# An f32 encoder layer on one core: rows for the MLP turned in 32x32 blocks by VectorE instead of by TensorE transposes

## The chip, the core and the metric

The kernel runs on one core of one Trainium2 chip. Its time is the device time of one execution in microseconds (us); the median of several runs is given, with the lowest and highest. A core has five engines that matter here, each with a queue of its own that it runs in order: TensorE (PE in the profile; its weight loads are PEld), VectorE (DVE), ScalarE (ACT), GpSimd (POOL) and SyncE (SP, which only issues transfers). ScalarE and GpSimd issue transfers too.

## The reference

One layer over two sequences, a prompt of 1024 rows and a sample of 512 rows, 1024 wide, all in f32:

```
xn = RMSNorm(x);  z = xn @ W_in -> q_A,k_A,v_A,q_B,k_B,v_B,gate_A,gate_B
A  = grouped-query attention (8 heads of 64, 2 key heads), 2-D rotary
B  = 2-D neighbourhood attention, learned position bias
x  = x + (sigmoid(gate_A) * (o_A @ W_pA) + sigmoid(gate_B) * (o_B @ W_pB)) @ W_out
x  = x + relu(RMSNorm(x) @ W_up)^2 @ W_down          (1024 -> 4096 -> 1024)
out = RMSNorm(x)
```

The change touches the RMSNorm ahead of the MLP and the way its result gets from rows to columns: `RMSNorm(x) @ W_up` needs the normalised rows with the 1024 features on the partitions, while the norm itself has rows on the partitions.

## The kernel before

Every f32 product is made of three products of a reduced form (`mm3`): each operand is cut in a high part (a copy by ScalarE) and a low part (x minus the copy, by VectorE), and hi·hi, hi·lo and lo·hi are added up in PSUM. So each operand tile costs one ScalarE pass and one VectorE pass.

The two sequences go one after the other through the same phases (`run`, one `Trunk` each: s0 is the sample, s1 the prompt): projections and attention A, attention B, and a last phase with the merge and the product with W_out. Then `mlp` runs over all 1536 rows, in two blocks of 768 rows. Its up projection uses a Strassen-Winograd scheme: the activation block is cut in 2x2 parts, of which seven combinations `B[0]` to `B[6]` are made once per block, and seven combinations of the weights (`A`, from sums called `S`) for each of the blocks of the 4096 features. The seven products go to the PSUM banks `ua`, `ub`, `uc`, `ud`.

The last phase of a trunk works on tiles of 128 rows, in two column halves. In half 1 each tile ends like this: TensorE finishes `ops` (the product with W_out), VectorE adds the residual (`hs`, L1389), and `norm_tile` makes the normalised tile: ScalarE squares and sums, VectorE scales the mean (`ms_hs`, L176), GpSimd takes the power (`rs_hs`, L180), and VectorE multiplies row by its factor and by the gain (`xnhs`, one SCALAR_TENSOR_TENSOR over 128x1024, L291). GpSimd stores the tile to a DRAM buffer `hnd`.

- In s0 the phase has four tiles, and each round also normalises one tile of the next trunk: `xnns`, the same steps, which TensorE then turns with eight transposes into `ptxs` (`p0_t`, L315); ScalarE and VectorE cut that into `xs_0h` and `xs_0l` (L331). The next trunk's projections (`zs`, weights `wghs` and `wgls`) begin right behind.
- In s1 there are eight tiles; the first four are normalised in the phase, the other four later, one at a time, inside the up loop of block 0 (`late_norm`).

`hnd` is read back on SP's queue, two tiles of 128 rows at a time (rows j and j+3 of a block of six), and `pair_t` makes one column strip of all seven `B[i]` from such a pair: 16 TensorE transposes (L355) turn the two tiles into four PSUM banks (`pt`), ScalarE copies one of them aside (`y`, L372), VectorE makes the four temporaries `ta` (L377 to L383), and ScalarE and VectorE (two of the low parts GpSimd) write the high and low parts (L364, L367). Block 0's three pairs are made in rounds 3 to 5 of s1's last phase, between the products with W_out; block 1's three pairs between block 0's and block 1's up loops, beside the first down products (`dnf`).

A scheduler (the Tile framework) turns the program into one order per engine, with semaphores where a value or a buffer is waited for, from its own estimates; the order in the code is a starting point for it. Names in the profile leave out the buffer numbers.

Of the kernel before, what the change touches and what calls it, by code (L numbers as in the profile page):

```python
# [11 lines left out]
F32 = mybir.dt.float32  # L12
# [49 lines left out]
def encoder(ctx: ExitStack, tc: tile.TileContext, xs, outs, w):  # L62
# [217 lines left out]

    def norm_tile(src, gb, pool, nm, tag="xn", bufs=2, pin=False, between=None):

        xn = pool.tile([P, D], F32, tag=tag, name=f"xn{nm}", bufs=bufs)
        ss = sml.tile([P, 8], F32, tag="ss", name=f"ss{nm}")
        op = nc.scalar.activation(xn, src, AF.Square, accum_out=ss[:, 0:1])
        if pin:
            tc.keep_in_program_order(op)
        r = rstd(ss[:, 0:1], 1, D, nm, pin)
        if between is not None:
            between()  # L290
        op = nc.vector.scalar_tensor_tensor(xn, src, r[:, 0:1], gb, op0=ALU.mult, op1=ALU.mult)  # L291
        if pin:
            tc.keep_in_program_order(op)
        return xn

    def norm_to(xn, src, gb, nm, pin=False):
# [4 lines left out]
        r = rstd(ss[:, 0:1], 1, D, nm, pin)  # L301
        op = nc.vector.scalar_tensor_tensor(xn, src, r[:, 0:1], gb, op0=ALU.mult, op1=ALU.mult)
        if pin:
            tc.keep_in_program_order(op)
        return xn
# [43 lines left out]

    def pair_t(nm, j, tiles, B, banks, tmp):  # L350

        b11, b21, b12, b22 = banks
        for halves, t in (((b11, b21), tiles[0]), ((b12, b22), tiles[1])):
            for c in range(NC8):
                nc.tensor.transpose(  # L355
                    halves[c // 4][:, (c % 4) * P : (c % 4 + 1) * P], t[:, c * P : (c + 1) * P], ident
                )
        cols = slice(j * P, (j + 1) * P)

        def v(t):  # L360
            return t.rearrange("p (k c) -> p k c", c=P)

        def hi(i, src):
            nc.scalar.activation(B[i][:, 0, :, cols], v(src), AF.Copy)  # L364

        def lo(i, src, eng=nc.vector):
            eng.tensor_tensor(B[i][:, 1, :, cols], v(src), B[i][:, 0, :, cols].bitcast(F32), op=ALU.subtract)  # L367

        y1 = tmp(f"y1{nm}")
        a2, a1, a3, a4 = (tmp(f"ta{i}{nm}") for i in (2, 1, 3, 4))  # L370
# [9 lines left out]
        nc.vector.tensor_tensor(a3, b22, y1, op=ALU.subtract)  # L380
# [40 lines left out]
    def run(tr, nxt, first):  # L421
# [854 lines left out]
        with phase(f"phG{N}") as ph:  # L1276
# [5 lines left out]
            def tmp_zs(name):  # L1282
                return ph.tile([P, 512], F32, tag="zs", name=name, bufs=6 if nxt is not None else 8)

            def hn_raw(j):
                res = []
                for t in (j, j + 3):
                    r = rawp.tile([P, 1024], F32, tag="raw", name=f"hn0_{t}")
                    nc.sync.dma_start(r, hnd[t * P : (t + 1) * P, :])
                    res.append(r)  # L1290
                return res

            def pool_wp(shape, dt, name):
                return ph.tile(shape, dt, tag="k4", name=name, bufs=4)

# [46 lines left out]
            for half in range(2):  # L1342
                wo = wos[half]
                hc = slice(half * 512, half * 512 + 512)
                for tt in range(NT):
# [6 lines left out]
                    if later:  # L1352
                        xr = ph.tile([P, D], F32, tag="k4", name=f"xr{nm}", bufs=4)[:, 0:512]
                    else:
                        xr = tmp_zs(f"xr{nm}")
                    nc.sync.dma_start(xr, x[tt * P : (tt + 1) * P, hc])
                    ht = hs_[tt // 2][:, tt % 2, :] if tb == 0 else None
                    if ht is None and half == 1 and not later:
                        ht = ph.tile([P, D], F32, tag="k4", name=f"ht{nm}", bufs=4)
                        nc.sync.dma_start(ht[:, 0:512], hd[rows_, 0:512])  # L1360
                    if half == 1 and nxt is not None:
                        xt = ph.tile([P, D], F32, tag="k4", name=f"xa{nm}", bufs=4)
                        nc.sync.dma_start(xt, nxt.x[tt * P : (tt + 1) * P, :])
# [36 lines left out]
                    if half == 1:  # L1400
                        if later:
                            late_norms.append(r0)
                        else:
                            hn = norm_tile(ht, gb, ph, f"h{nm}", "k4", 4)
                            nc.gpsimd.dma_start(hnd[rows_, :], hn)
                        if nxt is not None:

                            if tt < NT - 1:
                                ahead.append((tt, norm_tile(xt, gn, ph, f"n{nm}", "k4", 4)))
                            else:  # L1410
                                xn = slot_left([P, D], F32, f"xnn{nm}")
                                nxt.carry.append((tt, norm_to(xn, xt, gn, f"n{nm}")))
                        else:
                            if tt == 2:
                                hn_t = hn_raw(0)
                            if tt == 3:

                                right.close()
# [5 lines left out]
                            if 3 <= tt <= 5:  # L1424
                                j = tt - 3
                                if j == 2:
# [3 lines left out]
                                    first_a0.append(a0)  # L1430
                                both = [big(f"pt0_{j}_{i}") for i in range(2)]
                                banks = [b_[:, q * 512 : q * 512 + 512] for b_ in both for q in range(2)]
                                pair_t(f"0_{j}", j, hn_t, B0, banks, tmp_zs)
                                if j < 2:
                                    hn_t = hn_raw(j + 1)
            if nxt is not None:
                nxt.ready = NT

    def mlp():
# [27 lines left out]
        def hn_load(b, j):  # L1467
            res = []
            for t in (j, j + 3):
                r0 = b * BT + t * P  # L1470
                r = raw4(f"hn{b}_{t}")
                nc.sync.dma_start(r, hnd[r0 : r0 + P, :])
                res.append(r)
            return res
# [300 lines left out]
        for q in range(3):  # L1775
            if q < 2:
                for g in range(2):
                    a_dma(5, g, q + 1)
            pair_t(f"1_{q}", q, hn.pop(q), B, [bank(f"pt1_{q}_{i}") for i in range(4)], t2)
            if q < 2:  # L1780
# [208 lines left out]
```

## Time and profile before

| | |
|---|---|
| median of 3 runs | 2117.03 us (2116.83 to 2118.7) |
| the profiled execution | 2116.56 us, of which its span is 2114.6 us |
| granted TensorE clock | 0.999 of full speed |
| `pair_t`: TensorE transposes | 96, in six groups of 16 |
| tiles normalised for the MLP | 12: four in s0's last phase (from 357 us), four in s1's (from 1132 us), four in block 0's up loop |

In the tables that follow, a group row gives line, engine, operation, output <- inputs, shapes and count, then busy time and mean ns of one, then the idle time of the engine just before these instructions and what ended most of it. A timeline row gives start, duration (both us), engine, line, operation; a bracket at its end is the idle time before it and its releaser. Matmuls overlap in the pipeline, so TensorE's work is read from start to start. A row of a stretch gives its window, its length, and then the busy time and count of TensorE, its weight loads, VectorE, ScalarE and GpSimd, and the granted clock, the share of the transfer engines and GB/s. A row for L1094 by length gives the count, then shortest, median and longest in ns.

### The profile page before, as it was taken

Reading aid. Unit: us, or ns where it says so; the run is one execution under the profiler, and the core shown is the slowest. Engines: PE = TensorE matmul, PEld = TensorE weight load, DVE = VectorE, ACT = ScalarE, POOL = GpSimd, SP = SyncE. Lnnn points to the kernel's source line nnn. Section 1 sums busy time; section 2 is a strip of 40 time slices with the busy share of each in tenths; the row PEclk is TensorE's granted clock in tenths of the full one; section 3 lists DMA queues with packets and bytes.
Section 4 is the critical chain, followed back from the end, with each engine's and each line's share of the span. In section 5 each row is a group of like instructions: output and inputs, shape, how many; then the busy total and the mean of one; then the engine's idle time right before and its main releaser. Section 6 shows DMA issues by size and latency. Waiting matters only on the chain.

```text
span 2114.6 us, 31728 instructions
## 1 busy us (share of the span) xinstructions
PE 2092.2 (99%) x10871; PEld 1838.6 (87%) x10871; DVE 1478.7 (70%) x2793; ACT 1146.4 (54%) x2487; POOL 361.8 (17%) x446
## 2 busy tenths in 40 slices
PE   9999999999999999999999999999999999999998
PEld 8888788988898888888888999999999988888887
DVE  6665786777647756778863877777777777669563
ACT  6664653667566645556522566566555633334442
POOL 2232310333233314543101100012000000000000
PEclk9999999999999999999999999999999999999999
DMA  6437557530132136776563565478444899688561
GB/s 192 135 104 213 147 168 253 177 85 26 55 83 69 43 99 196 234 238 200 166 218 133 184 200 197 156 234 221 154 160 146 281 354 338 214 280 279 156 208 61
DMA packets 336104, 372.92 MB, mean 176 GB/s; under 512 B 31039, under 2 KB 267207, under 8 KB 335943
## 3 DMA queue, kind: packets, MB, share of 16 engines
q1 hardware_dynamic: 297463, 305.60, 45.9%
q10 hardware_dynamic: 31328, 45.11, 6.4%
q0 software_dynamic: 7152, 20.19, 3.5%
q8 instruction: 86, 1.41, 0.3%
q14 instruction: 75, 0.61, 0.1%
HBM read 274.29 MB, written 97.32 MB: 176 GB/s over the span
## 4 chain that ended last, share of the span: by engine, by line
PE 78%; DVE 1%; issue 1%; ACT 0%; POOL 0%; DMA 0%; POOLq 0%; DVEq 0%; ACTq 0%
PE dn L214 20%; PE gpss L214 8%; PE ud L214 6%; PE ua L214 6%; PE uc L214 6%; PE ops L214 3%; PE ub L214 3%; PE pTs L835 3%; PE zs L214 2%; PE ppbs L214 2%; PE pqbs L214 2%; PE pkbs L214 2%; PE ppas L214 2%; PE zvs L214 2%; PE dnf L214 2%; PE os L811 1%
## 5 line engine op out<-in xcount | busy, mean ns | idle before, releaser
L214 PE MATMUL dn<-wd,ah 128*128 128x512 f32 x1248 | 384.1, 389 | 0.0
L214 PEld LDWEIGHTS dn<-wd,ah 128*128 128x128 f32 x1248 | 234.3, 188 | 48.3
L214 PE MATMUL dn<-wd,al 128*128 128x512 f32 x624 | 242.8, 389 | 0.0
L1463 ACT ACTIVATE ah<-ar 128x512 fp32r<-128x512 f32 x168 | 104.5, 628 | 208.4 <-PE dn L214 193.2
L214 PE MATMUL gpss<-xs_0h,w_gs 128*128 128x512 f32 x512 | 189.6, 402 | 0.7 <-DVE ot_Bs L477 0.4
L1464 DVE TENSOR_TENSOR al<-ar,ah 128x512 fp32r<-128x512 f32 x168 | 114.2, 686 | 78.6 <-ACT ah L1463 71.3
L214 PE MATMUL ud<-B,A 128*128 128x384 f32 x768 | 143.6, 334 | 0.7 <-DVE c L1581 0.7
L214 PE MATMUL uc<-B,A 128*128 128x384 f32 x768 | 143.7, 334 | 0.0
L214 PE MATMUL ua<-B,A 128*128 128x384 f32 x768 | 138.8, 334 | 0.0
L214 PEld LDWEIGHTS dn<-wd,al 128*128 128x128 f32 x624 | 117.2, 188 | 24.5
L799 POOL TENSOR_SCALAR ps<-ps,rls 128x1024 f32<-128x1024 f32 (+1 forms) x96 | 97.4, 1016 | 227.6 <-DVE rls L798 209.6
L214 PEld LDWEIGHTS ud<-B,A 128*128 128x128 f32 x768 | 133.9, 188 | 1.0 <-DVE c L1581 1.0
L214 PEld LDWEIGHTS uc<-B,A 128*128 128x128 f32 x768 | 134.0, 188 | 0.2 <-ACT A L1463 0.2
L214 PEld LDWEIGHTS ua<-B,A 128*128 128x128 f32 x768 | 133.7, 188 | 0.2
L841 DVE TENSOR_TENSOR ptls<-pTs,pths 128x512 fp32r<-128x512 f32 x160 | 107.8, 686 | 36.5 <-ACT pths L840 35.5
L840 ACT ACTIVATE pths<-pTs 128x512 fp32r<-128x512 f32 x160 | 94.3, 598 | 69.1 <-PE pTs L835 66.6
L214 PE MATMUL ops<-wh_os,mgs 128*128 128x512 f32 x384 | 119.5, 391 | 0.0
L793 DVE TENSOR_REDUCE nms<-ss 128x1 f32<-128x1024 f32 (+1 forms) x96 | 99.4, 1039 | 20.1 <-PE ss L791 19.0
L214 PEld LDWEIGHTS gpss<-xs_0h,w_gs 128*128 128x128 f32 x512 | 96.1, 188 | 18.9 <-DVE w_gs L208 0.7
L796 ACT ACTIVATE ps<-ss,nms 128x1024 f32<-128x1024 f32 (+1 forms) x96 | 93.3, 972 | 31.5 <-DVE nms L793 29.0
L180 POOL TENSOR_TENSOR rs_f<-ms_f,mhalf 128x1 f32<-128x1 f32 x6 | 4.0, 666 | 590.7 <-DVE ms_f L176 590.7
L835 PEld LDWEIGHTS pTs<-ident,ps 128*128 128x128 f32 x640 | 78.3, 140 | 27.6 <-POOL ps L799 4.0
(287 smaller groups left out, 5137.9 us busy)
## 6 DMA issues: line engine op xcount, KB each, us to landing
ar<-ud SPq DMA_DIRECT2D x120, 512.0 KB, 5.1
br<-in_w_mlp_down_dram SPq DMA_DIRECT2D x72, 512.0 KB, 5.4
rawu<-in_w_mlp_up_dram SPq DMA_DIRECT2D x64, 512.0 KB, 4.1
ud<-c ACTq DMA_DIRECT2D x128, 192.0 KB, 2.9
raw_gs<-in_w_in_dram SPq DMA_DIRECT2D x32, 512.0 KB, 3.9
ud<-cs SPq DMA_DIRECT2D x64, 192.0 KB
tbs<-pbs SPq DMA_DIRECT2D x24, 384.0 KB, 4.6
bhs<-tbs SPq DMA_DIRECT2D x24, 384.0 KB, 3.8
```

The source lines that it names most:

```text
L180: op = nc.gpsimd.tensor_tensor(r[:, :n], m[:, :n], mhalf[:, :n], op=ALU.pow)
L214: op = nc.tensor.matmul(out, a, b, **kw)
L793: nc.vector.tensor_reduce(nm_, s, axis=AX.X, op=ALU.max, negate=True)
L796: op = nc.scalar.activation(p, s, AF.Exp, bias=nm_, accum_out=l)
L799: nc.gpsimd.tensor_scalar(p, p, rl, 1.0, op0=ALU.mult, op1=ALU.mult)
L811: nc.tensor.matmul(o, vhl[:, kc, :], lo, start=False, stop=(kc == NT - 1))
L835: nc.tensor.transpose(pt[:, j * P : (j + 1) * P], PP[u, j][:, kc * P : (kc + 1) * P], ident)
L840: nc.scalar.activation(hi, pt, AF.Copy)
L841: nc.vector.tensor_tensor(lo, pt, hi.bitcast(F32), op=ALU.subtract)
L1463: nc.scalar.activation(hi, src, AF.Copy)
L1464: nc.vector.tensor_tensor(lo, src, hi.bitcast(F32), op=ALU.subtract)
```

## The change

The 96 transposes go. A tile is turned in two steps. VectorE turns each 32x32 block in place with a STREAM_TRANSPOSE (`turned`), and the load that reads the tile back from `hnd` puts the blocks in their places (`turned_rows`): it takes pieces of 256 f32 (1 KB), 512 of them, where it took 128 whole rows of 4 KB. So that each piece holds what one partition needs, the scaling pass of the norm now reads its row and the gain with a stride of four f32 (`blocked`) and writes contiguously. `pair_t` reads the loaded tiles directly, in runs of 32 elements; its banks and the copy `y` are gone. All twelve tiles are turned so. Around it, the loads for block 0 are issued in rounds 1 to 3, into two kinds of buffers; the last phase of s1 has five buffers of the kind `k4` (four before), and six of the kind `zs` (eight before).

```
-    def norm_tile(src, gb, pool, nm, tag="xn", bufs=2, pin=False, between=None):
+    def blocked(t, natural):
+        return t.rearrange("p (c i b) -> p b c i" if natural else "p (b c i) -> p b c i", b=4, i=32)
+
+    def norm_tile(src, gb, pool, nm, tag="xn", bufs=2, pin=False, between=None, turn=False):
...
+        if turn:
+            nc.vector.scalar_tensor_tensor(
+                blocked(xn, False), blocked(src, True), r[:, 0:1], blocked(gb, True), op0=ALU.mult, op1=ALU.mult
+            )
+            turned(xn)
+            return xn
...                                                    (the same in norm_to)
-    def pair_t(nm, j, tiles, B, banks, tmp):
-
-        b11, b21, b12, b22 = banks
-        for halves, t in (((b11, b21), tiles[0]), ((b12, b22), tiles[1])):
-            for c in range(NC8):
-                nc.tensor.transpose(
-                    halves[c // 4][:, (c % 4) * P : (c % 4 + 1) * P], t[:, c * P : (c + 1) * P], ident
-                )
+    def turned(xn):
+
+        blocks = xn.rearrange("p (n i) -> p n i", i=32)
+        nc.vector.transpose(blocks, blocks)
+
+    def turned_rows(r0):
+        return hnd[r0 : r0 + P, :].rearrange("(a i) (b w) -> (i b) a w", i=32, b=4)
+
+    def pair_t(nm, j, tiles, B, tmp):
+
+        (b11, b21), (b12, b22) = (
+            [t.rearrange("p (a c t) -> p c a t", a=4, c=8)[:, 4 * h : 4 * h + 4] for h in range(2)] for t in tiles
+        )
...
-        nc.scalar.activation(y1, b12, AF.Copy)
...
-        nc.vector.tensor_tensor(a1, y1, b11, op=ALU.subtract)
+        nc.vector.tensor_tensor(a1, b12, b11, op=ALU.subtract)
...
-            def hn_raw(j):
-                res = []
-                for t in (j, j + 3):
-                    r = rawp.tile([P, 1024], F32, tag="raw", name=f"hn0_{t}")
-                    nc.sync.dma_start(r, hnd[t * P : (t + 1) * P, :])
...
+            def hn_raw(j, e):
+                if j and e:
+                    r = ph.tile([P, D], F32, tag="k4", name=f"hn0_{j}_{e}", bufs=nk4)
+                else:
+                    r = rawp.tile([P, 1024], F32, tag="raw", name=f"hn0_{j}_{e}")
+                nc.sync.dma_start(r.rearrange("p (a w) -> p a w", a=4), turned_rows((j + 3 * e) * P))
...
-                            hn = norm_tile(ht, gb, ph, f"h{nm}", "k4", 4)
+                            hn = norm_tile(ht, gb, ph, f"h{nm}", "k4", nk4, turn=True)
...
-                            if tt == 2:
-                                hn_t = hn_raw(0)
+                            if tt == 1:
+                                hn_raw(0, 0)
+                                hn_raw(0, 1)
+                                hn_raw(1, 0)
+                            if tt == 2:
+                                hn_raw(1, 1)
+                            if tt == 3:
+                                hn_raw(2, 1)
...                                                    (rounds 3 to 5; mlp)
-            norm_to(xn, hl.pop(r0), gl[0][:, 0, :], f"l{r0}")
+            norm_to(xn, hl.pop(r0), gl[0][:, 0, :], f"l{r0}", turn=True)
```

The engines' orders move with it at three places that matter. A name ends in half, tile and buffer number; `xnhs_1_0` is the normalised tile 0 of half 1.

VectorE's order in s0's last phase, before:

```order
L291 SCALAR_TENSOR_TENSOR xnhs_1_0_4455<-hs_0_4284,rs_hs_1_0_4460,gbms_4286 128x1024
L176 TENSOR_SCALAR ms_ns_1_0_4467<-ssns_1_0_4465 128x1
L1389 TENSOR_TENSOR hs_0_4284<-ops_1_1_4476,xrs_1_1_4472 128x512
L291 SCALAR_TENSOR_TENSOR xnns_1_0_4464<-xas_1_0_4426,rs_ns_1_0_4469,gns_4288 128x1024
L176 TENSOR_SCALAR ms_hs_1_1_4523<-sshs_1_1_4521 128x1
L291 SCALAR_TENSOR_TENSOR xnhs_1_1_4520<-hs_0_4284,rs_hs_1_1_4525,gbms_4286 128x1024
L176 TENSOR_SCALAR ms_ns_1_1_4532<-ssns_1_1_4530 128x1
L331 TENSOR_TENSOR xs_0l_4503<-ptxs_0_4505,xs_0h_4501 128x4x128
L331 TENSOR_TENSOR xs_0l_4504<-ptxs_0_4505,xs_0h_4502 128x4x128
L291 SCALAR_TENSOR_TENSOR xnns_1_1_4529<-xas_1_1_4474,rs_ns_1_1_4534,gns_4288 128x1024
```

and after:

```order
L295 SCALAR_TENSOR_TENSOR xnhs_1_0_4455<-hs_0_4284,rs_hs_1_0_4460,gbms_4286 128x1024
L176 TENSOR_SCALAR ms_ns_1_0_4468<-ssns_1_0_4466 128x1
L368 STREAM_TRANSPOSE xnhs_1_0_4455<-xnhs_1_0_4455 128x1024
L300 SCALAR_TENSOR_TENSOR xnns_1_0_4465<-xas_1_0_4426,rs_ns_1_0_4470,gns_4288 128x1024
L1411 TENSOR_TENSOR hs_0_4284<-ops_1_1_4477,xrs_1_1_4473 128x512
L176 TENSOR_SCALAR ms_hs_1_1_4524<-sshs_1_1_4522 128x1
L295 SCALAR_TENSOR_TENSOR xnhs_1_1_4521<-hs_0_4284,rs_hs_1_1_4526,gbms_4286 128x1024
L346 TENSOR_TENSOR xs_0l_4504<-ptxs_0_4506,xs_0h_4502 128x4x128
L346 TENSOR_TENSOR xs_0l_4505<-ptxs_0_4506,xs_0h_4503 128x4x128
L368 STREAM_TRANSPOSE xnhs_1_1_4521<-xnhs_1_1_4521 128x1024
L176 TENSOR_SCALAR ms_ns_1_1_4534<-ssns_1_1_4532 128x1
L1411 TENSOR_TENSOR hs_1_4285<-ops_1_2_4543,xrs_1_2_4539 128x512
```

The turn stands ahead of `xnns`, the residual add of the next tile has moved behind `xnns`, and an add and two rows of the next projection's weights (`wgls`) now come ahead of the second `xnns`. On TensorE, the first group of `ptxs` transposes now stands behind five instead of ten matmuls of the third tile's `ops`, and the second behind nineteen instead of eight of the fourth's.

VectorE's order from the fourth tile of s1 to the first pair, before:

```order
L1389 TENSOR_TENSOR hs_1_12581<-ops_1_3_12960,xrs_1_3_12958 128x512
L176 TENSOR_SCALAR ms_hs_1_3_12990<-sshs_1_3_12988 128x1
L291 SCALAR_TENSOR_TENSOR xnhs_1_3_12987<-hs_1_12581,rs_hs_1_3_12992,gbms_12582 128x1024
L367 TENSOR_TENSOR B_0_13000<-pt_0_0_13012,B_0_13000 128x4x128
L377 TENSOR_TENSOR ta_0_13032<-y_0_13030,pt_0_0_13012 128x512
```

and after:

```order
L368 STREAM_TRANSPOSE xnhs_1_2_12957<-xnhs_1_2_12957 128x1024
L396 TENSOR_TENSOR ta_1_13080<-hn_1_1_12967,hn_1_0_12926 128x512
L1411 TENSOR_TENSOR hs_1_12585<-ops_1_3_12971,xrs_1_3_12969 128x512
L398 TENSOR_TENSOR ta_1_13079<-hn_1_1_12967,ta_1_13080 128x512
L176 TENSOR_SCALAR ms_hs_1_3_13001<-sshs_1_3_12999 128x1
L295 SCALAR_TENSOR_TENSOR xnhs_1_3_12998<-hs_1_12585,rs_hs_1_3_13003,gbms_12586 128x1024
L368 STREAM_TRANSPOSE xnhs_1_3_12998<-xnhs_1_3_12998 128x1024
L387 TENSOR_TENSOR B_0_13014<-hn_0_0_12922,B_0_13014 128x4x128
L387 TENSOR_TENSOR B_4_13018<-hn_0_1_12924,B_4_13018 128x4x128
```

One temporary of the second pair (`ta_1`) has come ahead of the add, a second one behind it; the first pair's rows follow the last turn.

TensorE's order at the end of that tile, before:

```order
L214 MATMUL ops_1_3_12960<-wh_os_1_4_12627,mgs_0_4_1_12395 128x512
L355 MATMUL pt_0_0_13012<-ident,hn_0_12954 128x128 x8
L355 MATMUL pt_0_1_13013<-ident,hn_3_12956 128x128 x8
L214 MATMUL ops_1_4_13060<-wh_os_1_0_12615,mgs_1_0_0_12235 128x512
L214 MATMUL ops_1_4_13060<-wl_os_1_0_12616,mgs_1_0_0_12235 128x512
```

and after:

```order
L214 MATMUL ops_1_3_12971<-wl_os_1_4_12632,mgs_0_4_0_12398 128x512
L214 MATMUL ops_1_3_12971<-wh_os_1_4_12631,mgs_0_4_1_12399 128x512
L214 MATMUL ops_1_4_13052<-wh_os_1_0_12619,mgs_1_0_0_12239 128x512
L214 MATMUL ops_1_4_13052<-wl_os_1_0_12620,mgs_1_0_0_12239 128x512
```

The two groups of eight transposes are gone from between the products of two tiles; nothing takes their place.

More of the change, by code (lines that the diff above doesn't have):

```diff
@@ L294, in norm_tile, with norm_to @@
         return xn
-    def norm_to(xn, src, gb, nm, pin=False):
+    def norm_to(xn, src, gb, nm, pin=False, turn=False):
         ss = sml.tile([P, 8], F32, tag="ss", name=f"ss{nm}")
@@ L301, in norm_to @@
         r = rstd(ss[:, 0:1], 1, D, nm, pin)
+        if turn:
+            nc.vector.scalar_tensor_tensor(
+                blocked(xn, False), blocked(src, True), r[:, 0:1], blocked(gb, True), op0=ALU.mult, op1=ALU.mult
+            )
+            turned(xn)
+            return xn
         op = nc.vector.scalar_tensor_tensor(xn, src, r[:, 0:1], gb, op0=ALU.mult, op1=ALU.mult)
@@ L376, in pair_t @@
         lo(0, b11)
[L377 removed]
+        nc.vector.tensor_tensor(a1, b12, b11, op=ALU.subtract)
         hi(2, a1)
         nc.vector.tensor_tensor(a2, b22, a1, op=ALU.subtract)
[L380 removed]
+        nc.vector.tensor_tensor(a3, b22, b12, op=ALU.subtract)
         hi(3, a3)
@@ L1352, in run @@
                     if later:
-                        xr = ph.tile([P, D], F32, tag="k4", name=f"xr{nm}", bufs=4)[:, 0:512]
+                        xr = ph.tile([P, D], F32, tag="k4", name=f"xr{nm}", bufs=nk4)[:, 0:512]
                     else:
@@ L1408, in run @@
                             if tt < NT - 1:
-                                ahead.append((tt, norm_tile(xt, gn, ph, f"n{nm}", "k4", 4)))
+                                ahead.append((tt, norm_tile(xt, gn, ph, f"n{nm}", "k4", nk4)))
                             else:
@@ L1430, in run @@
                                     first_a0.append(a0)
[L1431 to L1435, printed above, removed]
+                                pair_t(f"0_{j}", j, [hn_t[j][e] for e in range(2)], B0, tmp_zs)
+                                if j == 0:
+                                    hn_raw(2, 0)
             if nxt is not None:
@@ L1471, in hn_load @@
                 r = raw4(f"hn{b}_{t}")
-                nc.sync.dma_start(r, hnd[r0 : r0 + P, :])
+                nc.sync.dma_start(r.rearrange("p (a w) -> p a w", a=4), turned_rows(r0))
                 res.append(r)
@@ L1778, in mlp @@
                     a_dma(5, g, q + 1)
-            pair_t(f"1_{q}", q, hn.pop(q), B, [bank(f"pt1_{q}_{i}") for i in range(4)], t2)
+            pair_t(f"1_{q}", q, hn.pop(q), B, t2)
             if q < 2:
```

27 lines of the change are left out of this document (15 added, 12 removed).

## The prediction

> **What bounds the kernel now.** I read the busy shares first, then the chain that ended last.
>
> ```profile
> PE 2092.2 (99%) x10871; PEld 1838.6 (87%) x10871; DVE 1478.7 (70%) x2793; ACT 1146.4 (54%) x2487; POOL 361.8 (17%) x446
> PE 78%; DVE 1%; issue 1%; ACT 0%; POOL 0%; DMA 0%; POOLq 0%; DVEq 0%; ACTq 0%
> ```
>
> TensorE is busy 99% of the span of 2114.6 us, and of the chain's attributed time nearly all is its own. So TensorE work taken out counts in full, as long as nobody is late to TensorE at that place; VectorE work put in counts only where TensorE waits for VectorE. The case is therefore decided at the places where the new VectorE work lies.
>
> **What is removed.** The 96 transposes of `pair_t`, in six groups of 16. Their price is read from the starts of the matmuls around them, since a busy time of pipelined work overlaps its neighbours.
>
> ```profile
> L355 PE MATMUL pt<-ident,hn 128*128 128x128 f32 x96 | 11.6, 273 | 0.0
> 1148.29 0.40 PE L214 MATMUL ops<-wh_os,mgs 128*128 128x512 f32 x1
> 1148.52 1.91 PE L355 MATMUL pt<-ident,hn 128*128 128x128 f32 x16
> 1150.19 0.47 PE L214 MATMUL ops<-wh_os,mgs 128*128 128x512 f32 x1
> 1150.50 0.39 PE L214 MATMUL ops<-wl_os,mgs 128*128 128x512 f32 x1
> 1158.02 0.39 PE L214 MATMUL ops<-wl_os,mgs 128*128 128x512 f32 x1
> 1158.40 1.94 PE L355 MATMUL pt<-ident,hn 128*128 128x128 f32 x16
> 1424.07 1.91 PE L355 MATMUL pt<-ident,hn 128*128 128x128 f32 x16
> 1425.74 0.70 PE L214 MATMUL dnf<-wd,ah 128*128 128x512 f32 x2
> ```
>
> A matmul starts every 0.23 (1148.29 to 1148.52). From 1148.52 to 1150.50 stand 16 transposes and one matmul: 1.98 − 0.23 = 1.75. The second group starts 0.38 after the last matmul, 0.15 more than the pitch. Six groups: 6 x 1.75 + 0.15 = **10.6 us off TensorE**. From below 6 x 1.67 = 10.0 (1424.07 to 1425.74), from above the busy time of the group, 11.6. The 1.67 is 0.104 for one transpose.
>
> [...]
>
> `pair_t` also drops its ScalarE copy (y1) and waits for nothing from TensorE now; both lie beside TensorE work and are costed at nothing, for ScalarE is 54% busy.
>
> **What is added, per turned tile.** (a) The scaling pass (SCALAR_TENSOR_TENSOR, below STT) reads both sources at a stride of four f32, 16 bytes; (b) a new 32x32 STREAM_TRANSPOSE of 128x1024 on VectorE. Twelve tiles, four each in three places.
>
> ```profile
> L291 DVE SCALAR_TENSOR_TENSOR xnhs<-hs,rs_hs,gbms 128x1024 f32<-128x1024 f32 x8 | 10.3, 1285 | 5.3 <-POOL rs_hs L180 5.3
> L1106 DVE STREAM_TRANSPOSE pbs<-pbs 128x768 f32<-128x768 f32 x24 | 23.2, 966 | 0.0
> L1389 DVE TENSOR_TENSOR hs<-ops,xrs 128x512 f32<-128x512 f32 x16 | 10.8, 687 | 23.5 <-PE ops L214 23.5
> L1094 ACT ACTIVATE pbs<-sbss,nmbs x50: 596/616/997, 793.3 to 970.8; 128x384 f32<-128x384 f32 x50
> L1094 ACT ACTIVATE pbs<-sbss,nmbs x14: 978/990/1016, 977.6 to 1027.1; 128x384 f32<-128x384 f32 x14
> ```
>
> (b): 966 ns at 768 elements, plus 256 x 1.17 ns ((1285 − 687)/512): 1.26 us, and 1.18 from start to start.
>
> (a): no row shows a strided read on VectorE. Nearest is ScalarE's L1094, the same operation in two forms: written contiguously 616 ns (median), written at 16 bytes' stride 990. That is 374/384 = 0.97 ns more per element, a second element time. Bounds: nothing (STT stays 1.29), or each of the two sources pays it apart (1.29 + 2 x 1.0 = 3.28). I take one such price, **STT = 2.28**, because that row is the nearest.
>
> [...]
>
> Each tile then costs VectorE 1.0 + 1.18 = 2.2 us more.
>
> **Place 1: the first trunk's w_out phase (345 to 395), where TensorE transposes the next trunk's tiles (`ptxs`) close behind VectorE.**
>
> ```profile
> 345.00:395.00 50.00, 49.20 (x264) 43.05 (x263) 34.22 (x60) 26.37 (x64) 12.40 (x21) 1.00 0.70 234
> 357.18 0.69 DVE L1389 TENSOR_TENSOR hs<-ops,xrs 128x512 f32<-128x512 f32 x1 [2.63 <-PE ops L214]
> 360.00 1.29 DVE L291 SCALAR_TENSOR_TENSOR xnhs<-hs,rs_hs,gbms 128x1024 f32<-128x1024 f32 x1 [0.70 <-POOL rs_hs L180]
> 363.00 1.28 DVE L291 SCALAR_TENSOR_TENSOR xnns<-xas,rs_ns,gns 128x1024 f32<-128x1024 f32 x1
> 364.46 1.04 PE L315 MATMUL ptxs<-ident,xnns 128*128 128x128 f32 x8
> 367.70 1.29 DVE L331 TENSOR_TENSOR xs_0l<-ptxs,xs_0h 128x512 fp32r<-128x512 f32 x2
> 370.52 1.09 PE L315 MATMUL ptxs<-ident,xnns 128*128 128x128 f32 x8 [0.24 <-DVE xnns L291]
> 370.98 2.48 DVE L208 TENSOR_TENSOR wgls<-rawqs,wghs 128x512 fp32r<-128x512 f32 x4
> 386.20 1.06 PE L315 MATMUL ptxs<-ident,xnns 128*128 128x128 f32 x8 [0.21 <-DVE xnns L302]
> ```
>
> TensorE is busy 49.2 of 50 here, yet two of the four `ptxs` groups already wait 0.2 for VectorE (the brackets): there is no slack for it. Replayed with the new order, add to STT being 2.82 (357.18 to 360.00):
>
> - Tile 0: STT 360.0 to 362.3, turn to 363.5, `xnns` to 364.8. TensorE reaches `ptxs` at 363.3 (five matmuls of 0.23 earlier than 364.46 by the order): waits 1.5.
> - Tile 1: the add now stands behind `xnns` and starts at 364.7; STT 367.5 to 369.8; then two `xs_0l` (1.2), turn (1.2, to 372.1), an add (0.6), two `wgls` (2.48/4 each), `xnns` 374.0 to 375.3. TensorE is there at about 374.2 (370.28, the 370.52 without its old wait, plus eleven matmuls of 0.227, plus 1.5, is 374.3): waits 1.2 (374.0 + 1.28 − 374.2, and a tenth for the hand-over).
> - The next projection's matmuls want `xs_0l` of tile 1, behind STT and an add of later tiles: 1.4. The same for tile 2, 0.75. After that VectorE is ahead again.
>
> **Lost: 1.5 + 1.2 + 1.4 + 0.75 = 4.9 us.** The same replay at STT = 1.29 gives 0.8, at 3.28 gives 9.0.
>
> **Place 2: end of the second trunk, up to the MLP's first products.** Before, S (VectorE) ends just in time for `ub`:
>
> ```profile
> 1132.40 0.69 DVE L1389 TENSOR_TENSOR hs<-ops,xrs 128x512 f32<-128x512 f32 x1 [4.75 <-PE ops L214]
> 1148.73 0.69 DVE L1389 TENSOR_TENSOR hs<-ops,xrs 128x512 f32<-128x512 f32 x1 [1.36 <-PE ops L214]
> 1151.53 1.28 DVE L291 SCALAR_TENSOR_TENSOR xnhs<-hs,rs_hs,gbms 128x1024 f32<-128x1024 f32 x1 [0.69 <-POOL rs_hs L180]
> 1154.02 0.69 DVE L367 TENSOR_TENSOR B<-pt,B 128x512 fp32r<-128x512 f32 x1 [1.20 <-ACT B L364]
> 1176.00 0.69 DVE L1396 TENSOR_TENSOR xrs<-ops,xrs 128x512 f32<-128x512 f32 x1 [2.32 <-PE ops L214]
> 1176.61 0.68 DVE L1525 TENSOR_TENSOR S<-rawu,rawu 128x512 f32<-128x512 f32 x1
> 1175.80 2.27 PE L214 MATMUL ua<-B,A 128*128 128x384 f32 x12
> 1178.80 0.62 PE L214 MATMUL ub<-B,A 128*128 128x384 f32 x2 [0.72 <-ACT A L1463]
> ```
>
> Tiles come every 5.44 ((1148.73 − 1132.40)/3). VectorE's own chain for one tile is 2.82 + STT + 1.2: 5.3 at an STT of 1.29, so it keeps up; 6.3 at 2.28, so it falls behind 0.9 a tile. The fourth add then starts at 1132.4 + 3 x 6.34 + 0.6 = 1152.0 instead of 1148.73, its turn ends at 1158.4. Behind that stand 25 rows of the pairs and of A (19 x 0.60 + 6 x 0.70 + 0.4 = 16.0) and the last add (0.6): S starts at 1175.0. TensorE meanwhile loses three groups: `ua` goes from 1175.80 to 1170.4, and S started 0.81 behind it, so it is wanted at 1171.2. **Lost: 3.75 us.** At 1.29 VectorE reaches the last add at 1170.0 and nothing is lost; at 3.28, 7.8.
>
> **Place 3: the second block's pairs, and the four tiles normalised inside the up loop.**
>
> ```profile
> 1223.68 0.56 DVE L1573 TENSOR_TENSOR cs<-c,c 128x384 f32<-128x384 f32 x1 [2.08 <-ACT c L1583]
> ```
>
> In the up loop VectorE sits idle 2.08 for each feed-forward block like this one; a turned tile adds 2.2 to one block in two: hidden. In the second block (from 1424.07) TensorE runs the `dnf` products while the pairs are made, and the pairs no longer need it; the row buffers are now held until VectorE has read them instead of until the transposes, which I put at 0 to 0.5. Taken as 0.
>
> **The read-back.** Its loads fetch 512 pieces of 1 KB where 128 rows of 4 KB were fetched.
>
> ```profile
> bhs<-tbs SPq DMA_DIRECT2D x24, 384.0 KB, 3.8
> hnd<-xnhs POOLq DMA_DIRECT2D x8, 512.0 KB, 3.6
> ```
>
> The nearest load from DRAM on that queue, `bhs`, lands in 3.8 us, and the store that must be through before it takes 3.6. In place 2 the loads are issued a tile or more ahead; costed at nothing, because VectorE is the later one there. The store waits on POOL's queue for the turn. Behind it stands the next tile's small `rstd`, which needs that tile's add first; only in place 1 is it the same round's `rs_ns`, free at about 372.7 for tile 1, still ahead of its `xnns` at 374.0.
>
> **Sum**, against the profiled run's own 2116.56 (span 2114.6 and 2.0 around it; the runs' median is 2117.03, 0.02% above): 2116.56 − 10.6 + 4.9 + 3.75 = **2114.6 us**, 0.09% faster. What a measurement of this kernel can tell from no change is about 0.2%, 4.2 us. The turned norms give back most of what the transposes free, and only because of the strided reads.
>
> **The rivals.**
>
> 1. *Strided reads cost nothing* (STT 1.29). Then VectorE keeps up at place 2, and place 1 loses 0.8: 2116.56 − 10.6 + 0.8 = 2106.8, faster by 0.46%. For it: the L1094 price is a write's, on another engine. Against it: it is the only stride in the trace, and it cost a full element time. Chance 0.22.
> 2. *Both sources pay* (STT 3.28), slower: VectorE becomes the bound of places 1 and 2. 2116.56 − 10.6 + 9.0 + 7.8 = 2122.8, slower by 0.29%. Losses grow by some 4.1 us at each place for each microsecond of STT, so the change is at zero with STT about 2.5 and 0.2% slower with about 3.1. For it: STT has two tensor sources, L1094 one strided side. Against: between 616 and 990 one side paid one price, and two reads may overlap. Chance 0.10.
> 3. *The read-back lands late*: at 10 us rather than 3.8, the second block's last pair would hold TensorE for about 2 us: 2114.6 + 2 = 2116.6. For it: four times the pieces. Against: 1 KB pieces still fill whole rows of the destination, and place 2 has them early. Chance 0.08.
> 4. *The transposes stay or move elsewhere*: excluded, for TensorE's order holds 96 fewer, and no other instruction of its queue takes their place.
>
> The likeliest case (one price) has 0.60; its own range is 2111 to 2118, for an STT between 1.9 and 2.6 at 8 us per microsecond over both places, plus 0.5 for the gross gain. About a quarter of it lies below 2112.3, the 0.2% mark.
>
> **How the numbers follow.** Faster by over 0.2%: rival 1 (0.22) and a quarter of the likeliest (0.15): 0.37. Slower: rival 2 (0.10) and what the likeliest and rival 3 leave above 2120.8 (0.02): 0.12. The rest 0.51. The range for 8 in 10 reaches to rival 1's 2106.5 below and to 2119 above; outside lie rival 2's upper part and half of rival 1.
>
> **What the profile after would show.** STT of the turned form at 2.3 (rival 1: 1.3; rival 2: 3.3), a transpose at 1.26, twelve of each. The 96 transposes and their group gone. `ptxs` waiting about 1.5 and 1.2 behind `xnns` in place 1, and `ub` waiting about 4 behind S near 1172, with VectorE busy without a gap for the 20 us before. If those waits are small although STT is 2.3, my replay of the queues is wrong; if STT is as taken and the read-back stands in the chain, rival 3. What would upset it most is the price of the stride, for both losses hang on it; next the order at place 1, where I followed each queue by hand.

## The result and the profile after

The changed kernel takes 2128.12 us (median of 6 runs, 2126.05 to 2130.95), the kernel before in the same comparison 2116.93 (2116.34 to 2118.7). The ratio is 1.0053, 95% interval 1.004 to 1.0066: **slower by 0.53%**, where 0.09% faster was forecast, and outside the range. The profiled execution has a span of 2126.5 us, 11.9 more than before.

The busy shares and the chain that ended last, after:

```profile
PE 2087.5 (98%) x10775; PEld 1833.0 (86%) x10775; DVE 1512.7 (71%) x2805; ACT 1142.9 (54%) x2481; POOL 368.9 (17%) x446
PE 41%; DVE 2%; DMA 1%; issue 1%; ACT 0%; POOL 0%; POOLq 0%; DVEq 0%; ACTq 0%
```

The 96 transposes are gone, yet the span grew: TensorE is busy 4.7 us less and idle 16.6 us more. In the chain VectorE has gone from 1% to 2% and the transfers from 0 to 1%. The view puts only 45% of the span down to an engine here, and 80% before, so its two shares of TensorE can't be compared.

The price of one turned tile was forecast well. Scaling pass and transpose (ns, shortest, median, longest):

```profile
L295 DVE SCALAR_TENSOR_TENSOR xnhs<-hs,rs_hs,gbms x8: 2029/2054/2105, 360.6 to 1158.6; 128x1024 f32<-128x1024 f32 x8
L368 DVE STREAM_TRANSPOSE xnhs<-xnhs x8: 1232/1245/1247, 362.7 to 1160.6; 128x1024 f32<-128x1024 f32 x8
```

2.05 us for the strided pass (2.28 taken, 1.29 without stride), 1.245 for the transpose (1.26 taken). The stride costs 0.77 us for 1024 elements, two sources read.

**Place 1**, the first trunk's last phase. TensorE's waits after (rows with a bracket):

```profile
365.12 1.09 PE L330 MATMUL ptxs<-ident,xnns 128*128 128x128 f32 x8 [1.04 <-DVE xnns L300]
375.87 1.09 PE L330 MATMUL ptxs<-ident,xnns 128*128 128x128 f32 x8 [1.24 <-DVE xnns L300]
381.58 0.44 PE L214 MATMUL zs<-wghs,xs_0l 128*128 128x384 f32 x1 [1.09 <-DVE xs_0l L346]
384.59 1.06 PE L330 MATMUL ptxs<-ident,xnns 128*128 128x128 f32 x8 [0.83 <-DVE xnns L300]
390.56 0.45 PE L214 MATMUL zs<-wghs,xs_0l 128*128 128x384 f32 x1 [0.73 <-DVE xs_0l L346]
```

With 0.21 at the last group they sum to 5.1; before, three waits summed to 0.8. Some 4.4 us are lost.

**Place 2**, the start of the MLP. VectorE from the last turn to S, GpSimd beside it, and TensorE (three timelines of the changed kernel):

```profile
1160.64 1.25 DVE L368 STREAM_TRANSPOSE xnhs<-xnhs 128x1024 f32<-128x1024 f32 x1
1161.81 4.32 DVE L387 TENSOR_TENSOR B<-hn,B 128x512 fp32r<-128x512 f32 x3
1166.65 2.84 DVE L387 TENSOR_TENSOR B<-ta,B 128x512 fp32r<-128x512 f32 x2
1171.22 2.38 DVE L387 TENSOR_TENSOR B<-hn,B 128x512 fp32r<-128x512 f32 x2
1182.54 0.68 DVE L1550 TENSOR_TENSOR S<-rawu,rawu 128x512 f32<-128x512 f32 x1
```

```profile
1163.01 2.56 POOL L387 TENSOR_TENSOR B<-ta,B 128x512 fp32r<-128x512 f32 x2
1177.97 6.38 POOL L387 TENSOR_TENSOR B<-ta,B 128x512 fp32r<-128x512 f32 x2 [1.70 <-ACT B L384]
```

```profile
1174.37 0.33 PE L214 MATMUL ua<-B,A 128*128 128x384 f32 x1
1176.66 2.21 PE L214 MATMUL ua<-B,A 128*128 128x384 f32 x11 [1.96 <-DVE B L387]
1185.67 1.01 PE L214 MATMUL ub<-B,A 128*128 128x384 f32 x2 [6.80 <-ACT A L1488]
1198.93 3.28 PE L214 MATMUL ud<-B,A 128*128 128x384 f32 x12 [2.67 <-DVE c L1606]
1206.89 2.24 PE L214 MATMUL ub<-B,A 128*128 128x384 f32 x12
```

Three rows of VectorE that would take 1.9 us take 4.3, pairs of rows 2.4 and 2.8 instead of 1.3, and two rows of GpSimd 6.4 instead of 2.7. TensorE waits 2.0, 6.8 and 2.7 us. In the kernel before, the same rows of GpSimd stood beside rows of VectorE that read PSUM (VectorE and GpSimd, before):

```profile
1169.23 2.71 POOL L367 TENSOR_TENSOR B<-ta,B 128x512 fp32r<-128x512 f32 x2 [1.09 <-ACT B L364]
...
1169.81 0.68 DVE L383 TENSOR_TENSOR ta<-pt,ta 128x512 f32<-128x512 f32 x1
1170.41 1.28 DVE L367 TENSOR_TENSOR B<-pt,B 128x512 fp32r<-128x512 f32 x2
1171.60 1.48 DVE L367 TENSOR_TENSOR B<-ta,B 128x512 fp32r<-128x512 f32 x2
```

There hardly a row was slowed: 0.60 from start to start with a source in PSUM, and only the two rows from `ta`, whose sources both lie in SBUF, took 0.2 longer (1.48 where two others took 1.28) as GpSimd's ended.

After TensorE's long wait its clock is lower, 0.50 from 1185 to 1188 and 1.00 again in the stretch from 1191. Stretches of the changed kernel (the columns behind the window: length; busy time and count of TensorE, its weight loads, VectorE, ScalarE, GpSimd; granted clock; transfer share; GB/s):

```profile
1180.00:1185.00 5.00, 0.00 (x0) 0.00 (x0) 4.96 (x8) 0.30 (x2) 5.00 (x4) 0.80 0.66 213
1185.00:1188.00 3.00, 2.33 (x7) 2.05 (x8) 2.94 (x6) 2.29 (x4) 1.46 (x3) 0.50 0.38 140
1188.00:1191.00 3.00, 3.00 (x14) 3.00 (x13) 0.65 (x2) 0.00 (x0) 0.00 (x0) 0.69 0.86 333
1191.00:1195.00 4.00, 4.00 (x25) 4.00 (x24) 3.12 (x6) 2.55 (x5) 0.00 (x0) 1.00 0.61 216
```

Between the first `ua` (1175.80 before, 1174.37 after) and the second `ub` (before in the first row below), the changed kernel loses 1.43 + 11.84 = **13.3 us**, where 3.75 was forecast. Longer waits are 10.0 of it (1.96 + 6.80 + 2.67, less the two of 0.72 that `ub` and `ud` had before). Another 3.0 are matmuls that start further apart: from `ub` to the group of eleven `uc` 4.34 instead of 2.94, from `ud` to `ua` 3.08 instead of 2.19, from there to the second `ub` 4.88 instead of 4.16. Two rows of before:

```profile
1195.05 2.24 PE L214 MATMUL ub<-B,A 128*128 128x384 f32 x12
1451.50 2.24 PE L214 MATMUL ub<-B,A 128*128 128x384 f32 x12
```

**Place 3**, block 1's pairs, after: VectorE, GpSimd and TensorE, and the piece of the chain that is the last read-back.

```profile
1429.92 1.78 DVE L402 TENSOR_TENSOR ta<-hn,ta 128x512 f32<-128x512 f32 x1
1431.63 1.78 DVE L387 TENSOR_TENSOR B<-hn,B 128x512 fp32r<-128x512 f32 x1
...
1429.50 3.36 POOL L387 TENSOR_TENSOR B<-ta,B 128x512 fp32r<-128x512 f32 x2 [105.69 <-ACT B L384]
...
1459.56 3.53 PE L214 MATMUL ua<-B,A 128*128 128x384 f32 x10 [2.62 <-DVE A L1489]
1462.92 2.26 PE L214 MATMUL ub<-B,A 128*128 128x384 f32 x12
...
1437.05 10.42 DMA hn<-hnd
```

The block's first `ub` is 11.42 late (1451.50 to 1462.92). It came in 11.84 late and the three groups saved here are 5.25, so **4.8 us** were lost where 0 was forecast. The load of the last pair stands 10.4 us in the chain.

The ledger against the span: −10.6 + 4.4 + 13.3 + 4.8 = 11.9. Each piece is good to about half a microsecond, so that it comes out to the tenth is chance. What is to be explained is places 2 and 3.

### The profile page after: what moved, and what is told of

Read it like the earlier page. It is cut to its first block, busy times and chain, and to the rows that moved or that the text cites. A ratio compares the mean times of both kernels' runs of the same rounds, so it can differ in the third digit from the quotient of the medians.

```text
span 2126.5 us, 31531 instructions
## 1 busy us (share of the span) xinstructions
PE 2087.5 (98%) x10775; PEld 1833.0 (86%) x10775; DVE 1512.7 (71%) x2805; ACT 1142.9 (54%) x2481; POOL 368.9 (17%) x446
```

## The experiments

Theory A: VectorE and GpSimd hold each other up when each reads two tensors from SBUF (at place 2 two rows of GpSimd took 6.4 us, 2.7 before); `pair_t` now reads its rows from SBUF instead of PSUM. Theory B: only the norms' added VectorE work costs. Theory C: the read-back is late. Ratios are to the kernel before.

### GpSimd's low parts by ScalarE

```
-        lo(2, a1, nc.gpsimd)
-        lo(3, a3, nc.gpsimd)
+        nc.scalar.activation(part(2, 1), a1, AF.Copy)
+        nc.scalar.activation(part(3, 1), a3, AF.Copy)
```

> The changed kernel, but the two low parts per pair that GpSimd makes are written by ScalarE as plain copies (their values are then wrong; VectorE's work stays the same). Theory A, VectorE and GpSimd hold each other up when both read two SBUF tensors: VectorE's rows of pair_t are all 0.68 us again, S of the MLP starts about 5 us earlier, TensorE's waits at the start of the MLP fall from 8.8 to about 3.5 us and at block 1 from 2.8 to about 1.5, the time is about 2119. Theory B, only VectorE's added work in the norms costs: nothing moves by more than 1 us, 2128. Theory C, the late read-back costs: 2128, and block 1 waits as before.

2118.02 us, ratio 1.0002 (0.9993 to 1.0011): 10.1 us below the changed kernel, as A said. VectorE and TensorE of this run:

```profile
1164.14 1.85 DVE L387 TENSOR_TENSOR B<-hn,B 128x512 fp32r<-128x512 f32 x3
1179.75 0.68 DVE L1550 TENSOR_TENSOR S<-rawu,rawu 128x512 f32<-128x512 f32 x1
...
1181.93 1.01 PE L214 MATMUL ub<-B,A 128*128 128x384 f32 x2 [2.94 <-ACT A L1488]
1195.77 4.21 PE L214 MATMUL ud<-B,A 128*128 128x384 f32 x12 [2.75 <-DVE c L1606]
```

From the end of the last turn to S, VectorE needs 15.6 us (1164.14 to 1179.75) instead of 20.7 (1161.81 to 1182.54), for the same 26 rows: 5.1 us were holding. The rest of the 10.1 follows from it or goes with it, for the edit also takes the two rows out of GpSimd's queue, where the residual stores stand behind them. At block 1 `ua` no longer waits at all, although the loads still come in 1 KB pieces.

### Read-back in whole rows

```
-        return hnd[r0 : r0 + P, :].rearrange("(a i) (b w) -> (i b) a w", i=32, b=4)
+        return hnd[r0 : r0 + P, :].rearrange("p (a w) -> p a w", a=4)
```

> The changed kernel, but the tiles are read back in whole rows of 4 KB instead of 512 pieces of 1 KB (values wrong, every engine's order the same). Theory C: the loads of block 1's last pair land in about 5 us instead of 10.4, the loss of 4.9 us around block 1's start goes: about 2123.5. Theories A and B: 2128, within 1 us.

2126.42 us, ratio 1.0042 (1.003 to 1.0055). Its interval overlaps the changed kernel's, and the 2123.5 of theory C was not reached; the wait at block 1's `ua` fell from 2.62 to 1.74. But the landing that the expectation counted on did not come: the last load stands in this run's chain with 9.30 us in whole rows, against 10.42 in pieces. So the run tests the pieces and not the late landing; they add at most a part of place 3. The late landing by itself is answered by act_lo: its last load takes 10.15 us in the chain, and `ua` doesn't wait.

### The pairs alone, the norms alone

The first is the changed kernel with norms as before and the rows read back whole; the second the kernel before with the turned norms, its transposes kept:

```
-                            hn = norm_tile(ht, gb, ph, f"h{nm}", "k4", nk4, turn=True)
+                            hn = norm_tile(ht, gb, ph, f"h{nm}", "k4", nk4)
...
-            norm_to(xn, hl.pop(r0), gl[0][:, 0, :], f"l{r0}", turn=True)
+            norm_to(xn, hl.pop(r0), gl[0][:, 0, :], f"l{r0}")
```

```
-                            hn = norm_tile(ht, gb, ph, f"h{nm}", "k4", 4)
+                            hn = norm_tile(ht, gb, ph, f"h{nm}", "k4", 4, turn=True)
...
-            norm_to(xn, hl.pop(r0), gl[0][:, 0, :], f"l{r0}")
+            norm_to(xn, hl.pop(r0), gl[0][:, 0, :], f"l{r0}", turn=True)
```

> The changed kernel without the turned norms: norms as before, rows read back whole, no transposes anywhere (values wrong). What is left of the change is pair_t reading SBUF tiles instead of PSUM. Theory A: the held VectorE rows are still there and take back about half of the 10.6 us: 2111 to 2113. Theory B: the whole gain is seen, 2106.3. Theory C: 2106.3 too.

2118.26 us, ratio 1.0003 (0.9994 to 1.0011). **Without any turned norm, the whole gain is gone**: more than theory A expected, and B and C (2106.3) are out as its cause. GpSimd and VectorE of this run, then TensorE:

```profile
1160.99 2.99 POOL L387 TENSOR_TENSOR B<-ta,B 128x512 fp32r<-128x512 f32 x2 [0.52 <-ACT B L384]
1170.70 6.37 POOL L387 TENSOR_TENSOR B<-ta,B 128x512 fp32r<-128x512 f32 x2 [1.70 <-ACT B L384]
...
1160.42 2.42 DVE L387 TENSOR_TENSOR B<-ta,B 128x512 fp32r<-128x512 f32 x2
1162.76 1.77 DVE L387 TENSOR_TENSOR B<-hn,B 128x512 fp32r<-128x512 f32 x1
...
1178.40 1.01 PE L214 MATMUL ub<-B,A 128*128 128x384 f32 x2 [4.03 <-ACT A L1488]
```

GpSimd's two rows take 6.4 us there beside rows of VectorE that follow each other without a gap, and at 0.60 us each from 1164.5 to 1176. The single row at 1162.76 took 1.77 while two rows of GpSimd ran (1160.99 to 1163.98). So here the one engine is held and there the other; what decides it no run shows.

> The kernel before with the turned norms added (strided scaling pass and the 32x32 transposes) and TensorE's 96 transposes kept (values wrong). Theories A and B: about 4.4 us lost in the first trunk's last phase, as in the changed kernel, and 0 to 1 at the start of the MLP, since VectorE has some 2 us of slack there: 2121 to 2122. If VectorE's added work by itself were the cause at the start of the MLP, it would be 2128 or more.

2125.51 us, ratio 1.0038 (1.0025 to 1.005): 7.6 above, more than the 4 to 5 expected. At place 1 the waits are those of the changed kernel; behind it TensorE's transposes of a pair wait 2.55 us for ScalarE, which waits for a turned norm's scaling pass (in norm_noturn, with the strided pass alone, such a wait took 1.9 us):

```profile
1165.70 2.36 PE L375 MATMUL pt<-ident,hn 128*128 128x128 f32 x16 [2.55 <-ACT B L384]
```

### The pairs alone without GpSimd, and with an earlier store

pair_only with the edit of act_lo:

> As pair_only (norms as before, no transposes, whole rows read back, values wrong), and GpSimd's two low parts per pair are written by ScalarE as copies. Theory A (VectorE and GpSimd hold each other up over SBUF): nothing is held, the whole 10.6 us shows, 2106 to 2108. If the loss in pair_only has another cause (the order, the late stores, the reading of SBUF itself): 2113 or more.

2111.83 us, ratio 0.9968 (0.9956 to 0.998): 6.4 below pair_only, so holding is the larger part, but 4 to 6 above the forecast. TensorE, and the chain ahead of its second wait:

```profile
1175.12 0.61 PE L214 MATMUL ub<-B,A 128*128 128x384 f32 x2 [0.72 <-ACT A L1488]
1187.52 4.21 PE L214 MATMUL ud<-B,A 128*128 128x384 f32 x12 [2.77 <-DVE c L1606]
...
1172.28 0.52 POOL hd L1419
1172.80 0.53 POOL gbl L1516
1173.33 6.41 DMA hd<-xrs
1179.76 0.64 ACT A L1488
```

The wait at S is gone. What is late next is a buffer: ScalarE's A waits for the last residual store (`hd<-xrs`), and the MLP's gain (`gbl`) is loaded ahead of it on GpSimd's queue. The next run changes that alone:

```
-                if st == (0, 0) and i == 1:
+                if st == (0, 1) and i == 1:
```

> pair_act (norms as before, no transposes, no work of GpSimd in pair_t, values wrong) with the load of the MLP's gain issued on GpSimd's queue after the last residual store instead of ahead of it. pair_act had 2106.5 as the full gain and came to 2111.8; its trace shows ScalarE's A waiting 2.6 us for that store, ud waiting 2.8 and then running at a lower clock. If the store's place in the queue is the cause, A is free some 2 us earlier and 3 to 4 us come back: 2107 to 2109. If not: 2111.8.

2108.56 us, ratio 0.9956 (0.9943 to 0.9968): 9.2 of the 10.6 us are back, `ud` waits 0.17 (`ub` still 2.02). So most of the gain existed, and two things took it: holding 6.4, and the store 3.3. The store stands in the changed kernel's own chain too, for 5.70 us ahead of the `ud` that waits 2.67 there; no run changes its place alone in that kernel.

### What the transposes cost

```
-        for halves, t in (((b11, b21), tiles[0]), ((b12, b22), tiles[1])):
+        for halves, t in (((b11, b21), tiles[0]), ((b12, b22), tiles[1])) * 2:
```

> The kernel before with each of the 96 transposes of pair_t issued twice, values right. It prices them: by the starts of the matmuls around them, 96 x 0.104 = 10.0 to 10.6 us more than before, 2128 to 2128.6. If TensorE had slack there or the transposes overlapped other work: clearly less than 10.

2127.55 us against 2117.76, ratio 1.0045 (1.0032 to 1.0058), 9.8 us by the medians and 7 to 12 by the interval: the 10.6 of the prediction lies in it.

### Stride and turn apart

From norm_only, first without the stride, then without the turn:

```
-                blocked(xn, False), blocked(src, True), r[:, 0:1], blocked(gb, True), op0=ALU.mult, op1=ALU.mult
+                xn, src, r[:, 0:1], gb, op0=ALU.mult, op1=ALU.mult
```

> norm_only with the scaling pass contiguous, so that of the turned norms only the 32x32 transposes are left (values wrong). norm_only was 7.6 us above before. If the transposes, 1.18 us a tile, are the larger part of VectorE's 1.95, and loss begins as soon as VectorE is late: 3 to 5 us above before, about 2122. By the replay of the prediction (0.8 at the first trunk's phase, 0 at the MLP's start): 2118.7.

2118.43 us, ratio 1.0003 (0.9994 to 1.0012): the replay's 2118.7, and the waits at place 1 sum to 1.6, 0.8 more than before, as in the replay.

```
         blocks = xn.rearrange("p (n i) -> p n i", i=32)
-        nc.vector.transpose(blocks, blocks)
+        return
```

> norm_only with the strided scaling pass and without the 32x32 transposes (values wrong): 0.77 us a tile more than before. By the replay, less than with the transposes alone: 2118 to 2119. If the stride is the main cause of norm_only's 7.6 us: 2122 or more.

2120.95 us, ratio 1.0013 (1.0004 to 1.0022), between the two expectations. The stride is the shorter addition, 0.77 us a tile against 1.18, and costs more (3.2 us against 0.7); both together cost 7.6, more than the sum, since VectorE's slack is used only once. The difference lies at place 1, where TensorE's waits sum to 4.3 with the stride alone and to 1.6 with the turn alone. Why isn't settled; the two runs differ in VectorE's order too.

### All three causes taken out

The changed kernel with the edits of norm_nostride, act_lo and pair_act_gl.

> The changed kernel with three suspected costs taken out together: the scaling pass contiguous, GpSimd's low parts by ScalarE as copies, and the gain's load behind the last residual store (values wrong). Left of the change: the 32x32 transposes and the read-back in 1 KB pieces. If the three are the whole cause, it is pair_act_gl's 2108.6 plus norm_nostride's 0.6: 2109 to 2111. If the transposes or the read-back cost more once VectorE has no slack: 2113 or more.

2109.74 us, ratio 0.9962 (0.995 to 0.9975), within the expectation. From the changed kernel (11.2 above before) to this one (8.1 below) 19.3 us come back, of the 21.8 up to the full gain of 10.6. So the three together are nearly the whole cause; how much of it each has in the changed kernel is shown for holding alone (act_lo). Against pair_act_gl the transposes and the read-back in pieces cost about 1 us together, no more than the noise.

### Versions with right values

```
-        lo(2, a1, nc.gpsimd)
-        lo(3, a3, nc.gpsimd)
+        lo(2, a1)
+        lo(3, a3)
```

> The changed kernel with GpSimd's two low parts per pair made by VectorE, values right. Theory A: nothing is held, but VectorE has six rows of 0.6 us more at each place, 3.6 us: act_lo's 2118 plus 3.6 at the start of the MLP and up to 0.5 at block 1, 2120 to 2123. Theory B: 2128 plus 3.6, about 2131.

The changed kernel, so edited: 2121.75 us, ratio 1.002 (1.001 to 1.0029), as expected: faster than the changed kernel, slower than before.

The next starts from the kernel before. `pair_t` takes each tile either through TensorE or turned:

```
+            if late[n]:
+                v = t.rearrange("p (a c t) -> p c a t", a=4, c=8)
+                quads.append([v[:, 4 * h : 4 * h + 4] for h in range(2)])
+                continue
             halves = [banks.pop(0) for _ in range(2)]
...
+            turn_ = [BT + t * P in late_norms for t in (q, q + 3)]
+            pair_t(f"1_{q}", q, hn.pop(q), B, banks, t2, turn_, nc.vector)
```

> The kernel before, where only the four tiles normalised inside the up loop are turned by VectorE (stride and turn hidden there); their 32 transposes at block 1 go, the other 64 stay; block 1's low parts are all VectorE's, values right. Theory A: 32 x 0.109 = 3.5 us gained, 0 to 1 lost at block 1 to VectorE's six more rows: 2113.5 to 2114.5. Theory C (late read-back of 1 KB pieces): up to 2 us lost at block 1, 2115 to 2116.

Only the four tiles of the up loop turned, block 1's low parts on VectorE: 2114.83 us, ratio **0.9985 (0.9976 to 0.9994)**, faster than both kernels: 3.1 below the kernel before, the 3.5 us of 32 transposes less a little.

> As late_dve, but GpSimd keeps its two low parts per pair in block 1. Theory A: VectorE's rows with two SBUF sources are held at 1.2 to 1.8 us there, 1 to 2.5 us lost at the start of block 1: 2114.5 to 2116. If holding does not matter there: 2113.5, not above late_dve.

The same with GpSimd's two low parts kept: 2118.22, ratio 1.0 (0.9991 to 1.0009), 3.4 us above, more than expected. Block 1's `ua` in the two (late_dve, then late_pool):

```profile
1449.98 2.00 PE L214 MATMUL ua<-B,A 128*128 128x384 f32 x10 [0.48 <-DVE A L1500]
...
1452.43 2.43 PE L214 MATMUL ua<-B,A 128*128 128x384 f32 x10 [2.24 <-DVE A L1500]
```

Here, with right values and one choice of engine between them, that choice is worth all of the gain, and late_pool's VectorE has stretched rows again (1.78 us for a `ta` at 1443.93).

```
+            for q in range(4):
+                nc.vector.scalar_tensor_tensor(
+                    xn[:, 256 * q : 256 * q + 256].rearrange("p (c i) -> p c i", i=32),
+                    blocked(src, True)[:, q],            (now "p (c b i) -> p b c i")
...
+        for b in range(4):
+            nc.sync.dma_start(
+                r[32 * b : 32 * b + 32, :].rearrange("p (a w) -> p a w", a=4),
+                hnd[r0 : r0 + P, 256 * b : 256 * b + 256].rearrange("(a i) w -> i a w", i=32),
+            )
```

> A version with right values out of these findings: the scaling pass in four pieces read in runs of 32 elements (no 16-byte stride), all twelve tiles turned, read back by four loads per tile, all low parts of pair_t on VectorE, the gain's load behind the last residual store. all_off's level plus six VectorE rows at the MLP's start (3.6 us) and 0 to 1.5 at block 1: 2112.5 to 2116. If VectorE is the bound there in full: 2118.

2124.83 us, ratio 1.0033 (1.0021 to 1.0045): a miss. The four pieces take 1.67 us instead of 1.28, the new order makes a `ptxs` group wait 3.7 us at place 1, `ub` waits 5.10 (with the same six more rows it waits 6.50 in dve_lo), and block 1's `ua` waits 1.72 and 2.95, where 0 to 1.5 was expected:

```profile
383.30 1.94 PE L342 MATMUL ptxs<-ident,xnns 128*128 128x128 f32 x8 [3.70 <-DVE xnns L306]
1183.28 1.01 PE L214 MATMUL ub<-B,A 128*128 128x384 f32 x2 [5.10 <-ACT A L1504]
```

late_dve with the edit of pair_act_gl:

> late_dve (only the four late tiles turned, values right) with the gain's load behind the last residual store. The store did not hold TensorE up in late_dve: 2114.8, unchanged within 0.5.

2116.93, ratio 0.9995 (0.9986 to 1.0004): 2 us more than expected. In its profile `ub` waits 1.78 where late_dve's waits 0.72, so the later load is no help where the store was not late. This version can't be told from before, nor clearly from late_dve, whose small gain therefore rests on its one set of 11 executions.

## Why the prediction was wrong

- *10.6 us off TensorE*: right (twice).
- *STT 2.28, turn 1.26*: right in kind, 2.05 and 1.245. The price of the stride was the doubt the prediction stressed, and it was not where it failed: at 2.05 its own slope of 8 us per microsecond gives about 2112.7, further from what was measured. Rival 2 named the right sign for another reason; its STT of 3.28 did not come.
- *Place 1, 4.9*: right, 4.4, with the four waits where the replay had them, but partly by luck. At an STT of 2.05 the replay's slope gives 4.0, and a fifth wait, 0.83 at the third `ptxs` group, wasn't in it.
- *`pair_t` ... waits for nothing from TensorE now; both lie beside TensorE work and are costed at nothing*: this step failed. It looked at what was removed and not at where the remaining rows read. The 25 rows of place 2 were priced from the trace before, where most of them had a source in PSUM: 16.0 us, 16.6 with the last add. With act_lo these 26 take 15.6, in the changed kernel 20.7. What was put at nothing, that the rows now share SBUF with GpSimd, costs 5.1 us of VectorE at place 2 alone, and 10.1 us of the kernel's time with all that follows.
- *Place 2, 3.75*: mis-sized, 13.3. To the 5.1 us of holding come the store whose place on GpSimd's queue the prediction never followed (3.3 us in pair_act), and the slower matmuls at a lower clock after the long waits (3.0 us; the clock was 0.50 and then 0.69 from 1185 to 1191).
- *Place 3, 0*: mis-sized, 4.8, mostly holding: act_lo has no wait at its `ua`. Rival 3's late landing was seen (10.4 us), but its reason, the number of pieces, was not: whole rows took 9.3. And it holds up nothing by itself (act_lo, 10.15).
- *Hidden in the up loop*: right. In the changed kernel TensorE waits for nothing there, and late_dve lives on it.

What the traces show of holding: VectorE's rows with a source in PSUM took 0.60 us from start to start beside GpSimd's (before), single rows with both sources in SBUF 1.7 to 1.8 where GpSimd's was running already (the changed kernel, pair_only), and GpSimd's two rows 6.4 instead of 2.7 where VectorE's came without a gap. The trace before had a sign of it that was not weighed: of L367's rows on VectorE, the eighteen from `pt` took 674 to 692 ns, the twelve from `ta`, with both sources in SBUF, 677 to 1364.

## What to carry to other kernels

When operands move from PSUM to SBUF, look up who else reads SBUF at that place: here two-source instructions of VectorE and of GpSimd held each other up (1.78 us for a row of 0.68). Work taken from the bounding engine is won only up to the next late chain, so before counting it, list every chain that ends at that place (here VectorE's rows, and a store whose buffer is wanted) with its slack. Put added work where its engine is idle (turning the four late tiles alone paid; the three versions with right values that turned all twelve were slower than before).

## What the runs showed of the hardware

- Holding went both ways at place 3: one VectorE row took 1.78 us (1429.92) beside GpSimd rows that themselves took 1.7 each (two in 3.36) instead of 1.29. With GpSimd's rows taken out the VectorE rows of `pair_t` take 0.68 (act_lo).
- A scaling pass that reads two f32 sources at 16 bytes' stride (128x1024) took 2.05 us instead of 1.285, 1.6 times.
- TensorE's granted clock fell within the wait of 6.8 us that ended at 1185.67: it was 1.00 up to 1183, 0.51 from there to 1185, 0.50 on to 1189, and 1.00 again from 1190. After waits of 2.62 (clock 0.52 from 1461 to 1463, place 3) and 2.77 us (`ud` 4.21 instead of 2.35, clock 0.83 over 1180 to 1200, pair_act) it was low as well; after 1.74 (plain_back) and 2.16 (dve_lo) the ten `ua` matmuls took 2.03 and 2.00 us, as the 2.00 after a wait of 0.48 (late_dve), after 1.77 (pair_only) 2.50. So in these runs the length of the wait alone doesn't settle it.
